# The delta-rule state loop of a hybrid decoder layer: three chained products a chunk replaced by one product with precomputed 128-row maps

## The chip, the cores and the metric

The kernel runs on one core of a Trainium2 chip. The metric is the device time of one execution in microseconds (us); the median of three runs of the kernel before is 1048.08 us (1046.65 to 1048.11). Traces name the engines PE (TensorE, matrix products; PEld is its weight load), DVE (VectorE), ACT (ScalarE), POOL (GpSimd) and SP (SyncE, which issues transfers).

## What is computed

One layer on 512 tokens of width 2048, all in float32: RMSNorm, one wide input projection into three groups of heads, an output projection, and the residual sum. The change touches the first group only, 12 heads of 64 channels with a state of 64 x 64 each. Cut to what matters:

```
h = rms(x, norm_g);  pa, pb, pc = split(h @ w_in)
r, k, v, ga, wd, ad = split(token_shift(pa, mu_a))   # RWKV-7 heads
# kk: normalized key, a: rate in (0,1), w: decay; per head and token t:
sa    = -state @ kk_t
state = state * w_t + outer(sa, kk_t * a_t) + outer(v_t, k_t)
y_t   = state @ r_t
# then a norm over the 64 channels of a head, a bonus term, and a silu gate
# pb: causal pooling; pc: stick-breaking attention (q, k, v, gate)
out = x + concat(ya, yb, yc) @ w_out
```

## The kernel before

Nearly all of TensorE's work is dense: the input projection is made tile by tile (54 tiles of 128 columns after a first group of three), each from 16 blocks of the inner dimension, and every block takes three products of 128 x 128 weights with 512 tokens (high part by high part, high by low, low by high). In the trace these products write `pj`; those of the output projection at the end write `oacc`. ACT and DVE make the two parts `wh` and `wl` of each half tile of weights while the half before it is used.

Everything else is put between these dense products. The RWKV heads (in six pairs, `rwkv(p)`), the attention (`attention(p)`) and the pooling are Python generators. After each dense product `pump` asks each generator whether its next small product may be issued. The answer comes from a planner, `Pace`, which estimates when operands will be ready, and adds a margin: `MARGIN` (2.5) in general and `TIGHT` in the state loop. The order of TensorE's instructions is therefore fixed when the program is built; if the estimate was too early, TensorE stops at the small product until its operand is there, since products run in order. Vector work under `urgent()` is moved ahead in DVE's queue.

A pair's 512 tokens are eight chunks of 64. For each pair:

- Products of the keys `bk` with `amr` (decayed keys and, in its third and fourth part, decayed `r`) go to two `gm` banks, 8 products a half of the chunks; DVE masks them into `lt`, `amr` and `rx`.
- `lt` is inverted: 32 x 32 blocks go through DRAM, DVE substitutes row by row (`xblk`), and two rounds of small products (`q1`, `q2`) join the blocks. `done[("mid", p)]` then lets the next pair begin.
- `bk` is transposed to `bkt`, the values `v` to half of `uv`. The other half of `uv` holds the state.
- The state loop goes over the chunks. A chunk is three chained products (`wps`, `ups`, `sps`, all in one bank `wus`), each read by DVE before the next can run, and two products for the output `y`. POOL makes `se`, the decayed old state.

A bank of PSUM is taken by tag: `g` has three, `c` two, `y` one. `amr` and `lt` exist twice, for even and odd pairs.

Of the kernel before, what the change touches and what calls it, by code (L numbers as in the profile page):

```python
# [13 lines left out]
P = 128  # L14
# [39 lines left out]
MARGIN = 2.5  # L54
TIGHT = 0.5
AHEAD = 300
EVACUATE = 25
DL = 4.0
SCAN = 150
TP = 15  # L60

# [155 lines left out]
def hybrid_trunk_kernel(ctx: ExitStack, tc: tile.TileContext, x, xT, w_in, w_out, vecs, consts, up_w, pool_w, out):  # L217
# [79 lines left out]

    amr_flats = [rp.tile([P, NC_ * 4 * C], F32, tag=f"amr{i}", name=f"amr{i}") for i in range(2)]
    amrs = [a.rearrange("p (c a t) -> p c a t", c=NC_, a=4) for a in amr_flats]
    lt_flats = [rp.tile([P, NC_ * 2 * C], F32, tag=f"lt{i}", name=f"lt{i}") for i in range(2)]  # L300
# [17 lines left out]
    KQ = 4  # L318
    for pl, tag, parts in ((ap, "q2", 1), (ap, "k2", 1), (ap, "w30", 1), (rp, "bk", 2), (rp, "bkt", 2), (rp, "rx", 2),
                           (rp, "uv", 2), (None, "amr", 3), (ap, "w20", 1), (ap, "w21", 1)):  # L320
        if pl is None:
            xt = amr_flats[1][:, 0:parts * T].rearrange("p (k t) -> p k t", k=parts)
        else:
            xt = pl.tile([P, parts, T], F32, tag=tag, bufs=2 if tag in ("bk", "rx") else 1, name=name("x"))
# [67 lines left out]

    def need2(*tiles):
        def at():
            q = pace.slots.get("g", [])
            t = max([pace.ready.get(Pace.key(a), 0.0) for a in tiles] + [0.0])
            free = sorted([pace.read.get(k, 1e9) for k in q] + [0.0] * (BANKS["g"] - len(q)))
            return MARGIN + max(t, free[1])

        return at  # L400
# [151 lines left out]
    def rwkv(p):  # L552
        col = lambda v: vec[:, v + p:v + p + 1]
        amr_flat, amr, lt = amr_flats[p % 2], amrs[p % 2], lts[p % 2]
        while ("k", p) not in got or (p > 0 and not done.get(("mid", p - 1))):
            yield None
# [65 lines left out]

        rx = rp.tile([P, NC_, 2, C], F32, tag="rx", bufs=2, name=name("rx"))
        ms = strict.rearrange("p (o t) -> p o t", o=1)
        mi = incl.rearrange("p (o t) -> p o t", o=1)
        for half in range(2):
            cs = slice(4 * half, 4 * half + 4)
            yield need2(*([amr_flat, bk] if half == 0 else []))
            gs = [gb("gm"), gb("gm")]
            for j in range(4):  # L630
                cc = 4 * half + j
                for h, s, other in quad:
                    mm(gs[h][:, j * P:(j + 1) * P], bk[s, cc, :, :], amr[s, cc, h:4:2, :])
# [47 lines left out]

        yield soon(lt)


        xt = tmp("xt", NC_ * B)
        xt3 = xt.rearrange("p (c t) -> p c t", t=B)
        for h in range(2):
            dve.transpose(xt3[h * HD:h * HD + B], lt[h * HD:h * HD + B, :, h, 0:B])
        yield need(xt, tag="g")
# [6 lines left out]
        for h in range(2):  # L696
            r0 = h * HD + B
            dve.tensor_copy(out=w1[r0:r0 + B, :], in_=q1[r0:r0 + B, :NC_ * B])
        yield need(w1, tag="g")
# [5 lines left out]
        for h in range(2):  # L705
            r0 = h * HD
            dve.tensor_copy(out=lt[r0:r0 + B, :, h, B:C], in_=q2[r0:r0 + B, :NC_ * B].rearrange("p (c t) -> p c t", t=B))
# [6 lines left out]
        bkt = rp.tile([P, NC_, P], F32, tag="bkt", name=name("bkt"))  # L714
        for half in range(2):
            yield need(bk, tag="g")
            tr = gb("tr")
            for j in range(4):
                transpose(tr[:, j * P:(j + 1) * P], bk[:, 4 * half + j, :, :])
            act.copy(out=bkt[:, 4 * half:4 * half + 4, :], in_=tr.rearrange("p (c t) -> p c t", c=4))  # L720

# [18 lines left out]
        for cc in range(NC_):  # L740
            last = cc + 1 == NC_
            yield need(amr_flat, uv, tag="c", margin=TIGHT)
            wus = cb("wus")
            wps, ups, sps = wus[:, 0:P], wus[:, P:P + C], wus[:, 2 * P:3 * P]
            mm(wps, amr[:, cc, 0:2, :], uv[:, cc, :, :])
            wsb = rp.tile([P, C], F32, tag="wsb", bufs=2, name=name("wsb"))
            with urgent():
                dve.tensor_copy(out=wsb[lo, :], in_=wps[lo, 0:C])
                dve.tensor_copy(out=wsb[hi, :], in_=wps[hi, C:P])
                if not last:  # L750
                    se = rp.tile([P, C], F32, tag="se", bufs=2, name=name("se"))
# [6 lines left out]
            yps = ybank[:, (cc % 4) * P:(cc % 4 + 1) * P]  # L758
# [5 lines left out]
            if not last:  # L764
                mm(sps, bkt[:, cc, :], uv[:, cc, :, :])
                with urgent():
# [204 lines left out]

    spare = [rp.tile([P, 2, T], F32R, tag=t, bufs=2, name=name("first")) for t in ("bk", "rx")]

# [24 lines left out]
    for h, s, other in quad:  # L998
        for i in range(2):
            pool.memset(amrs[i][other, :, 2 + h, :], 0.0)  # L1000
            pool.memset(lts[i][s, :, 1 - h, :], 0.0)

    def begin():
# [139 lines left out]
```

## Time and profile before

| | |
|---|---|
| median of 3 runs | 1048.08 us |
| the profiled execution's own time | 1047.92 us |
| span of its trace | 1046.1 us |
| PE busy | 990.5 us (95%) |
| DVE, ACT, POOL busy | 677.9, 500.4, 225.6 us |

A busy PE is counted by modelled ends of the products, which overlap: dense products are recorded with some 400 ns each, yet follow each other at some 230 ns. What the engine could still save is therefore read in two ways: from the distance between starts in the timeline, and from the list of waits.

### The profile page before, as it was taken

The page shows a single profiled execution, that of the slowest core. Times are in us where ns is not written, and L with a number is a line of the kernel's source. Part 1 is how long each engine was busy: PE and PEld are TensorE (multiplying, and loading weights), DVE is VectorE, ACT ScalarE, POOL GpSimd, SP SyncE. Part 2 cuts the span into 40 slices and gives each one's busy share as a digit, 9 for nine tenths or more (in the row PEclk, how much of TensorE's full clock was granted, in tenths as well). Part 3 has the DMA queues.
Part 4 walks back from the last instruction along what each step waited for, and adds up shares of the span by engine and source line. Part 5 has one row for each costly group of instructions (what it writes and reads, how often), then busy time and mean ns, then how long its engine had stood idle before and what let it go on. Part 6 is the DMA issues. An engine that isn't in the chain of part 4 may idle for free.

```text
span 1046.1 us, 13931 instructions
## 1 busy us (share of the span) xinstructions
PE 990.5 (95%) x5084; PEld 789.5 (75%) x5084; DVE 677.9 (65%) x1393; ACT 500.4 (48%) x814; POOL 225.6 (22%) x296
## 2 busy tenths in 40 slices
PE   8999999898998899988999999989899999999998
PEld 6867867677776777776877777767767877888886
DVE  5369685679668795687957888487974566323232
ACT  5656645554455653745645556556552226222111
POOL 0124320233212422233212232134221221000000
PEclk8999999999999999999999999999999999999999
DMA  9522323131231323113231322313232336724241
GB/s 336 197 86 78 100 82 99 64 88 61 91 103 45 90 74 124 62 66 86 66 121 61 96 66 91 106 60 77 78 101 77 111 107 219 257 104 141 101 141 61
DMA packets 62228, 109.18 MB, mean 104 GB/s; under 512 B 29776, under 2 KB 31184, under 8 KB 62160
## 3 DMA queue, kind: packets, MB, share of 16 engines
q1 hardware_dynamic: 62160, 108.30, 31.0%
q8 instruction: 40, 0.66, 0.3%
q14 instruction: 28, 0.23, 0.1%
HBM read 98.84 MB, written 9.44 MB: 104 GB/s over the span
## 4 chain that ended last, share of the span: by engine, by line
PE 45%; DVE 27%; issue 13%; ACT 7%; POOL 5%; DMA 3%; SPq 0%; POOLq 0%; DVEq 0%
PE pj L378 21%; PE oacc L378 16%; DVE wl L211 4%; POOL e L211 3%; DVE n L211 3%; DVE pr L211 3%; DVE xblk L211 2%; DVE uv L211 2%; DVE u L211 2%; PE first L378 2%; ACT e L211 2%; DVE amr L211 2%; DMA lt<-in_x 1%; DVE w L211 1%; PE o L378 1%
## 5 line engine op out<-in xcount | busy, mean ns | idle before, releaser
L378 PE MATMUL pj<-hh,wl 128*128 128x512 f32 x864 | 346.0, 401 | 5.7 <-DVE wl L211 5.6
L378 PE MATMUL pj<-hh,wh 128*128 128x512 f32 x864 | 346.6, 401 | 0.1
L378 PE MATMUL pj<-hl,wh 128*128 128x512 f32 x864 | 345.9, 400 | 0.0
L211 DVE TENSOR_TENSOR wl<-raw,wh 128x1024 fp32r<-128x1024 f32 x140 | 176.3, 1259 | 159.9 <-ACT wh L211 156.0
L211 ACT CAST wh<-raw 128x1024 fp32r<-128x1024 f32 x140 | 146.5, 1046 | 246.3 <-PE oacc L378 121.5
L378 PEld LDWEIGHTS pj<-hh,wl 128*128 128x128 f32 x864 | 163.0, 189 | 40.1 <-DVE wl L211 8.1
L378 PEld LDWEIGHTS pj<-hh,wh 128*128 128x128 f32 x864 | 163.0, 189 | 34.8 <-issue 3.3
L378 PEld LDWEIGHTS pj<-hl,wh 128*128 128x128 f32 x864 | 162.9, 189 | 32.4 <-issue 2.1
L378 PE MATMUL oacc<-wl,yh 128*128 128x512 f32 x256 | 100.0, 391 | 0.0
L378 PE MATMUL oacc<-wh,yh 128*128 128x512 f32 x256 | 99.6, 389 | 0.0
L378 PE MATMUL oacc<-wh,yl 128*128 128x512 f32 x256 | 99.6, 389 | 0.0
L211 POOL TENSOR_SCALAR e<-e 128x512 f32<-128x512 f32 x28 | 48.3, 1726 | 211.4 <-ACT e L211 165.6
L211 POOL TENSOR_SCALAR se<-uv,ec 64x64 f32<-64x64 f32 x84 | 56.4, 672 | 100.5 <-DVE uv L211 95.3
L211 POOL TENSOR_TENSOR d<-u 128x512 f32<-128x512 f32 x25 | 39.4, 1575 | 130.8 <-DVE u L211 93.9
L378 PEld LDWEIGHTS oacc<-wh,yl 128*128 128x128 f32 x256 | 48.1, 188 | 10.3 <-issue 0.2
L378 PEld LDWEIGHTS oacc<-wl,yh 128*128 128x128 f32 x256 | 48.1, 188 | 10.2 <-issue 0.2
L378 PEld LDWEIGHTS oacc<-wh,yh 128*128 128x128 f32 x256 | 48.1, 188 | 9.9
L211 DVE TENSOR_TENSOR_SCAN n<-n,m 128x512 f32<-128x512 f32 (+3 forms) x48 | 41.0, 864 | 15.8 <-ACT n L211 15.6
L211 ACT ACTIVATE e<-e 128x512 f32<-128x512 f32 x50 | 31.5, 629 | 36.2 <-POOL e L211 35.7
L211 DVE TENSOR_TENSOR u<-pj,rstd 128x512 f32<-128x512 f32 x50 | 34.5, 690 | 19.5 <-PE pj L378 18.6
L211 DVE TENSOR_TENSOR pr<-xblk,nblk 128x60 f32<-128x60 f32 (+8 forms) x180 | 42.1, 234 | 4.9
L211 DVE TENSOR_TENSOR xblk<-xblk,pr 128x60 f32<-128x60 f32 (+8 forms) x180 | 40.7, 226 | 4.6
(203 smaller groups left out, 1313.4 us busy)
## 6 DMA issues: line engine op xcount, KB each, us to landing
raw<-in_w_in SPq DMA_DIRECT2D x108, 512.0 KB, 3.4
raw<-in_w_out SPq DMA_DIRECT2D x32, 512.0 KB, 3.5
lt<-in_x SPq DMA_DIRECT2D x8, 512.0 KB, 3.7
xr<-in_x SPq DMA_DIRECT2D x16, 256.0 KB, 6.7
out<-xr SPq DMA_DIRECT2D x16, 256.0 KB, 4.4
yin<-yd SPq DMA_DIRECT2D x14, 256.0 KB, 4.0
fr<-in_w_in SPq DMA_DIRECT2D x12, 256.0 KB, 7.5
nblk<-s SPq DMA_DIRECT2D x24, 128.0 KB
```

The source lines that it names most:

```text
L211: return call(*args, **kw)
L378: pe.matmul(o, lhsT, rhs, start=start, stop=stop)
```

## The change

The inverse, the rates and the output products of a chunk are multiplied out ahead of the loop. `amr` is transposed (`amt`) and multiplied by the inverse `lt` (bank `am`, copied to `amx`). For each chunk and head `amx` is multiplied with a tile `bx` (banks `gh`), and DVE adds the result back into `bx`, on one half of the partitions to the transposed keys and the masked products, on the other half to the identity (now the third part of `amr`) and the decayed `r`. `bx` then holds two maps of 128 rows, one that takes state and values of a chunk to the next state and one that takes them to the output. The loop is one product `s`, one product for `y`, and a scaling by DVE; `wsb`, `se` and the copies of `uv` are gone.

`amr` now exists once; `done[("inv", p)]` lets the next pair begin, and `done[("mid", p)]` lets it write `amr` and `bk`. The margin `TIGHT` is 0.8 in place of 0.5, and the joining and the new products use `QUICK`, 1.0, in place of 2.5. An attention pair waits for the one before it.

```diff
-TIGHT = 0.5
+TIGHT = 0.8
+QUICK = 1.0
-TP = 15
+TP = 16
...
-        while ("k", p) not in got or (p > 0 and not done.get(("mid", p - 1))):
+        while ("k", p) not in got or (p > 0 and not done.get(("inv", p - 1))):
...
-        while p > 1 and not done.get(("rwkv", p - 2)):
+        while (p > 0 and not done.get(("mid", p - 1))) or (p > 1 and not done.get(("rwkv", p - 2))):
             yield None
...
-        dve.tensor_tensor(amr[lo, :, 2, :], r3[lo], e[lo, :, 1:], ALU.mult)
-        pool.tensor_tensor(amr[hi, :, 3, :], r3[hi], e[hi, :, 1:], ALU.mult)
+        dve.tensor_tensor(amr[:, :, 3, :], r3, e[:, :, 1:], ALU.mult)
...
+        for half in range(2):
+            yield need(bk, tag="g")
+            tr = gb("tr")
+            for j in range(4):
+                transpose(tr[:, j * P:(j + 1) * P], bk[:, 4 * half + j, :, :])
+            act.copy(out=bx[:, 4 * half:4 * half + 4, 0, :, :], in_=tr.rearrange("p (c h t) -> p c h t", c=4, h=2))
...
+        amt = rp.tile([P, NC_, P], F32, tag="bk", bufs=2, name=name("amt"))
+        for half in range(2):
+            yield need(amr_flat, tag="g")
+            tr = gb("at")
+            for j in range(4):
+                transpose(tr[:, j * P:(j + 1) * P], amr[:, 4 * half + j, 0:2, :])
+            act.copy(out=amt[:, 4 * half:4 * half + 4, :], in_=tr.rearrange("p (c t) -> p c t", c=4))
...
+        amx = rp.tile([P, NC_, P], F32, tag="bk", bufs=2, name=name("amx"))
+        for half in range(2):
+            yield need(lt, amt, tag="c", margin=QUICK)
+            g = cb("am")
+            for j in range(4):
+                cc = 4 * half + j
+                mm(g[:, j * P:(j + 1) * P], lt[:, cc, :, :], amt[:, cc, :])
+            act.copy(out=amx[:, 4 * half:4 * half + 4, :], in_=g.rearrange("p (c t) -> p c t", c=4))
+        for half in range(2):
+            cs = slice(4 * half, 4 * half + 4)
+            yield need2(amx, bx, tag="c", margin=QUICK)
+            gs = [cb("gh"), cb("gh")]
+            for j in range(4):
+                cc = 4 * half + j
+                for h, s, other in quad:
+                    mm(gs[h][:, j * P:(j + 1) * P], amx[s, cc, :], bx[s, cc, :, h, :])
+            with urgent():
+                for h, s, other in quad:
+                    g4 = gs[h].rearrange("p (c a t) -> p c a t", c=4, a=2)
+                    dve.tensor_tensor(bx[other, cs, :, h, :], g4[other], bx[other, cs, :, h, :], ALU.add)
+                    dve.tensor_tensor(bx[s, cs, :, h, :], g4[s], amr[s, cs, 2:4, :], ALU.add)
         done[("mid", p)] = True
...
-            yield need(amr_flat, uv, tag="c", margin=TIGHT)
-            wus = cb("wus")
-            wps, ups, sps = wus[:, 0:P], wus[:, P:P + C], wus[:, 2 * P:3 * P]
-            mm(wps, amr[:, cc, 0:2, :], uv[:, cc, :, :])
...
-                dve.tensor_copy(out=wsb[lo, :], in_=wps[lo, 0:C])
-                dve.tensor_copy(out=wsb[hi, :], in_=wps[hi, C:P])
...
-                        pool.tensor_scalar(se[s, :], uv[s, cc, h, :], ec[s, cc:cc + 1], None, ALU.mult)
-            yield need(wsb, lt, tag="y" if cc % 4 == 0 else None, margin=TIGHT)
-            mm(ups, lt[:, cc, :, :], wsb)
+            yield need(bx, uv, tag="y" if cc % 4 == 0 else None if last else "c", margin=TIGHT)
+            if not last:
+                sps = cb("s")
+                mm(sps[:, 0:P], bx[:, cc, 0, :, :], uv[:, cc, :, :])
+                with urgent():
                     for h, s, o in quad:
+                        dve.tensor_scalar(uv[s, cc + 1, h, :], sps[s, h * C:(h + 1) * C], ec[s, cc:cc + 1], None, ALU.mult)
...
-            mm(yps, uv[:, cc, :, :], amr[:, cc, 2:4, :], True, False)
-            with urgent():
-                dve.tensor_copy(out=uv[lo, cc, 0, :], in_=ups[lo, :])
-                dve.tensor_copy(out=uv[hi, cc, 1, :], in_=ups[hi, :])
-            yield need(uv, margin=TIGHT + 0.1)
-            if not last:
-                mm(sps, bkt[:, cc, :], uv[:, cc, :, :])
-                with urgent():
-                    for h, s, o in quad:
-                        dve.scalar_tensor_tensor(uv[s, cc + 1, h, :], sps[s, h * C:(h + 1) * C], ec[s, cc:cc + 1], se[s, :], ALU.mult, ALU.add)
-            mm(yps, uv[:, cc, :, :], rx[:, cc, :, :], False, True)
+            mm(ybank[:, (cc % 4) * P:(cc % 4 + 1) * P], uv[:, cc, :, :], bx[:, cc, 1, :, :])
```

How TensorE's instructions stand in the state loop before the change: from the third chained product of one chunk of pair 0 (`sps`, a part of the bank `wus`) to the first of the next (`wps`).

```order
L378 MATMUL wus_2091<-uv_1617,bkt_1603 128x128
L378 MATMUL y_2044<-rx_710,uv_1617 128x128
L378 MATMUL pj_2129<-hh_104,wh_2030 128x512
L378 MATMUL pj_2129<-hl_120,wh_2030 128x512
L378 MATMUL pj_2129<-hh_104,wl_2031 128x512
L378 MATMUL pj_2129<-hh_105,wh_2030 128x512
L378 MATMUL pj_2129<-hl_121,wh_2030 128x512
L378 MATMUL pj_2129<-hh_105,wl_2031 128x512
L378 MATMUL pj_2129<-hh_106,wh_2030 128x512
L378 MATMUL pj_2129<-hl_122,wh_2030 128x512
L378 MATMUL wus_2193<-uv_1617,amr_97 128x128
```

The same engine in the loop of the changed kernel, pair 1, a whole chunk.

```order
L380 MATMUL s_2989<-uv_2938,bx_1801 128x128
L380 MATMUL y_2993<-bx_1801,uv_2938 128x128
L380 MATMUL pj_2915<-hh_104,wl_2872 128x512
L380 MATMUL pj_2915<-hh_105,wh_2871 128x512
L380 MATMUL pj_2915<-hl_121,wh_2871 128x512
L380 MATMUL pj_2915<-hh_105,wl_2872 128x512
L380 MATMUL pj_2915<-hh_106,wh_2871 128x512
L380 MATMUL pj_2915<-hl_122,wh_2871 128x512
L380 MATMUL pj_2915<-hh_106,wl_2872 128x512
L380 MATMUL pj_2915<-hh_107,wh_2871 128x512
L380 MATMUL pj_2915<-hl_123,wh_2871 128x512
L380 MATMUL pj_2915<-hh_107,wl_2872 128x512
```

The row after these is the next chunk's `s`. Where eight dense products lay between one link of the chain and the next (nine at the other two links of a chunk), ten now do, and a chunk has one link in place of three.

DVE in the loop before the change, pair 0: one chunk's copies and its update of the state (each written x2, once for each head), with other work between them.

```order
L211 COPY wsb_2019<-wus_2017 64x64 x2
L211 TENSOR_TENSOR wl_2031<-raw_2028,wh_2030 128x1024
L211 COPY uv_1617<-wus_2017 64x64 x2
L211 SCALAR_TENSOR_TENSOR n_2005<-n_2005,m_2006 128x512
L211 TENSOR_TENSOR w_2000<-w_2000,n_2005 128x512
L211 SCALAR_TENSOR_TENSOR uv_1617<-wus_2017,ec_653,se_2022 64x64 x2
```

DVE in the changed kernel between the first and the second group of `gh` products of pair 1.

```order
L212 TENSOR_TENSOR wl_2872<-raw_2869,wh_2871 128x1024
L212 TENSOR_TENSOR e_2780<-e_2780,d_2141 128x512
L212 TENSOR_TENSOR bx_1801<-gh_2880,bx_1801 64x8x64
L212 TENSOR_TENSOR bx_1801<-gh_2880,amr 64x8x64
L212 TENSOR_TENSOR bx_1801<-gh_2881,bx_1801 64x8x64
L212 TENSOR_TENSOR bx_1801<-gh_2881,amr 64x8x64
L212 SCALAR_TENSOR_TENSOR qs_2799<-qm_2853,qs_2799 128x512
L212 SCALAR_TENSOR_TENSOR u_2788<-u_2788,vec,y_463_2856 128x512
L212 TENSOR_TENSOR bk_2951<-e_2780,e_2751 64x8x64
L212 TENSOR_TENSOR ck_2798<-u_2788,qs_2799 128x512
L212 TENSOR_TENSOR u_2913<-pj_2790,rstd 128x512
L212 TENSOR_TENSOR wl_2919<-raw_2916,wh_2918 128x1024
```

Six short instructions a chunk have left the loop, and four adds of 64 x 512 stand in one block behind each `gh` group, ahead of the next `wl`.

## Rows read from the trace of the kernel before

**Rows 1.** The page: span, and busy time of each engine with its share.

```profile
span 1046.1 us, 13931 instructions
...
PE 990.5 (95%) x5084; PEld 789.5 (75%) x5084; DVE 677.9 (65%) x1393; ACT 500.4 (48%) x814; POOL 225.6 (22%) x296
```

**Rows 2.** Waits of PE: who waited for whom, us in total, times, longest.

```profile
PE wus L378 <- DVE uv L211: 26.0, 24, 2.2
PE wus L378 <- DVE wsb L211: 6.4, 9, 1.2
PE pj L378 <- DVE wl L211: 5.6, 5, 1.9
...
PE y L378 <- DVE uv L211: 1.0, 1, 1.0
```

**Rows 3.** Timeline of PE, 314 to 320 us: start, us, instruction [idle before].

```profile
314.25 0.40 PE L378 MATMUL pj<-hh,wh 128*128 128x512 f32 x1
314.48 0.33 PE L378 MATMUL wus<-wsb,lt 128*128 128x64 f32 x2
314.64 0.44 PE L378 MATMUL y<-amr,uv 128*128 128x128 f32 x2
314.84 0.47 PE L378 MATMUL pj<-hl,wh 128*128 128x512 f32 x1
315.15 0.39 PE L378 MATMUL pj<-hh,wl 128*128 128x512 f32 x1
...
316.77 0.40 PE L378 MATMUL pj<-hh,wh 128*128 128x512 f32 x1
319.12 0.49 PE L378 MATMUL wus<-uv,bkt 128*128 128x128 f32 x2 [1.95 <-DVE uv L211]
```

**Rows 4.** Timeline of DVE in the same stretch.

```profile
316.70 1.22 DVE L211 TENSOR_TENSOR_SCAN c<-fresh,e 128x512 f32<-128x512 f32 x1
317.84 0.72 DVE L211 SCALAR_TENSOR_TENSOR sq<-d,vec,sq 128x512 f32<-128x512 f32 x1
318.59 0.47 DVE L211 COPY uv<-wus 64x64 f32<-64x64 f32 x2
```

**Rows 5.** Timeline of PE around four transposes of 128 x 128.

```profile
300.69 0.39 PE L378 MATMUL pj<-hh,wl 128*128 128x512 f32 x1
300.92 0.60 PE L382 MATMUL vt<-kon,d 128*128 128x128 f32 x4
...
301.59 0.39 PE L378 MATMUL qm<-sh,bmean_r 128*128 128x512 f32 x1
```

**Rows 6.** Timeline of PE around eight products of 64 rows each.

```profile
98.53 0.39 PE L378 MATMUL pj<-hh,wl 128*128 128x512 f32 x1
98.85 1.16 PE L378 MATMUL gm<-amr,bk 64*128 64x128 f32 x16
99.94 0.50 PE L378 MATMUL pj<-hh,wh 128*128 128x512 f32 x1
100.28 0.39 PE L378 MATMUL pj<-hl,wh 128*128 128x512 f32 x1
```

**Rows 7.** Groups of DVE by form: count, busy us, mean ns, idle before.

```profile
L211 DVE TENSOR_TENSOR wl<-raw,wh 128x1024 fp32r<-128x1024 f32 x140 | 176.3, 1259 | 159.9 <-ACT wh L211 156.0 <-PE pj L378 3.2
...
L211 DVE SCALAR_TENSOR_TENSOR uv<-wus,ec,se 64x64 f32<-64x64 f32 x84 | 23.7, 282 | 7.2 <-PE wus L378 5.2
L211 DVE COPY wsb<-wus 64x64 f32<-64x64 f32 x96 | 21.2, 220 | 17.9 <-PE wus L378 16.8
L211 DVE COPY uv<-wus 64x64 f32<-64x64 f32 x96 | 21.2, 220 | 7.0 <-PE y L378 4.9
...
L211 DVE TENSOR_TENSOR amr<-sq,E 64x512 f32<-64x512 f32 x12 | 10.5, 871 | 0.2
...
L211 DVE TENSOR_TENSOR q<-cq,q 64x512 fp32r<-64x512 f32 x12 | 8.2, 686 | 1.0 <-ACT q L211 0.7
```

**Rows 8.** Group of ACT: copies out of a bank of transposes.

```profile
L211 ACT COPY bkt<-tr 128x512 f32<-128x512 f32 x12 | 6.6, 589 | 14.4 <-PE tr L382 14.4
```

More of the change, by code (lines that the diff above doesn't have):

```diff
@@ L294, in load_constants @@
         dve.tensor_scalar(nvec[:, 12:13], vec[:, V_QN:V_QN + 1], HD ** -0.5, None, ALU.mult)
-    amr_flats = [rp.tile([P, NC_ * 4 * C], F32, tag=f"amr{i}", name=f"amr{i}") for i in range(2)]
-    amrs = [a.rearrange("p (c a t) -> p c a t", c=NC_, a=4) for a in amr_flats]
+    amr_flat = rp.tile([P, NC_ * 4 * C], F32, tag="amr", name="amr")
+    amr = amr_flat.rearrange("p (c a t) -> p c a t", c=NC_, a=4)
     lt_flats = [rp.tile([P, NC_ * 2 * C], F32, tag=f"lt{i}", name=f"lt{i}") for i in range(2)]
@@ L318, in hybrid_trunk_kernel @@
     KQ = 4
-    for pl, tag, parts in ((ap, "q2", 1), (ap, "k2", 1), (ap, "w30", 1), (rp, "bk", 2), (rp, "bkt", 2), (rp, "rx", 2),
+    for pl, tag, parts in ((ap, "q2", 1), (ap, "k2", 1), (ap, "w30", 1), (rp, "bk", 2), (rp, "bx", 4),
                            (rp, "uv", 2), (None, "amr", 3), (ap, "w20", 1), (ap, "w21", 1)):
         if pl is None:
-            xt = amr_flats[1][:, 0:parts * T].rearrange("p (k t) -> p k t", k=parts)
+            xt = amr_flat[:, 0:parts * T].rearrange("p (k t) -> p k t", k=parts)
         else:
-            xt = pl.tile([P, parts, T], F32, tag=tag, bufs=2 if tag in ("bk", "rx") else 1, name=name("x"))
+            xt = pl.tile([P, parts, T], F32, tag=tag, bufs=2 if tag in ("bk", "bx") else 1, name=name("x"))
         k = len(xk)
@@ L391, in need, with need2 @@
         return at
-    def need2(*tiles):
+    def need2(*tiles, tag="g", margin=MARGIN):
         def at():
-            q = pace.slots.get("g", [])
+            q = pace.slots.get(tag, [])
             t = max([pace.ready.get(Pace.key(a), 0.0) for a in tiles] + [0.0])
-            free = sorted([pace.read.get(k, 1e9) for k in q] + [0.0] * (BANKS["g"] - len(q)))
-            return MARGIN + max(t, free[1])
+            free = sorted([pace.read.get(k, 1e9) for k in q] + [0.0] * (BANKS[tag] - len(q)))
+            return margin + max(t, free[1])
         return at
@@ L553, in rwkv @@
         col = lambda v: vec[:, v + p:v + p + 1]
-        amr_flat, amr, lt = amr_flats[p % 2], amrs[p % 2], lts[p % 2]
-        while ("k", p) not in got or (p > 0 and not done.get(("mid", p - 1))):
+        lt = lts[p % 2]
+        while ("k", p) not in got or (p > 0 and not done.get(("inv", p - 1))):
             yield None
@@ L620, in rwkv @@
         yield soon(rs)
-        rx = rp.tile([P, NC_, 2, C], F32, tag="rx", bufs=2, name=name("rx"))
+        bx = rp.tile([P, NC_, 2, 2, C], F32, tag="bx", bufs=2, name=name("bx"))
         ms = strict.rearrange("p (o t) -> p o t", o=1)
@@ L632, in rwkv @@
                 for h, s, other in quad:
-                    mm(gs[h][:, j * P:(j + 1) * P], bk[s, cc, :, :], amr[s, cc, h:4:2, :])
+                    mm(gs[h][:, j * P:(j + 1) * P], bk[s, cc, :, :], amr[s, cc, h:4:3 - h, :])
             for h, s, other in quad:
@@ L682, in rwkv @@
         yield soon(lt)
+        done[("inv", p)] = True
         xt = tmp("xt", NC_ * B)
         xt3 = xt.rearrange("p (c t) -> p c t", t=B)
-        for h in range(2):
-            dve.transpose(xt3[h * HD:h * HD + B], lt[h * HD:h * HD + B, :, h, 0:B])
-        yield need(xt, tag="g")
+        with urgent():
+            for h in range(2):
+                dve.transpose(xt3[h * HD:h * HD + B], lt[h * HD:h * HD + B, :, h, 0:B])
+        yield need(xt, tag="g", margin=QUICK)
         q1 = gb("q1")
@@ L695, in rwkv @@
                 mm(q1[r0 + B:r0 + 2 * B, cc * B:(cc + 1) * B], lt[r0:r0 + B, cc, h, B:C], xt3[r0:r0 + B, cc, :])
[L696 to L699, printed above, removed]
+        with urgent():
+            for h in range(2):
+                r0 = h * HD + B
+                dve.tensor_copy(out=w1[r0:r0 + B, :], in_=q1[r0:r0 + B, :NC_ * B])
+        yield need(w1, tag="g", margin=QUICK)
         q2 = gb("q2")
@@ L704, in rwkv @@
                 mm(q2[r0:r0 + B, cc * B:(cc + 1) * B], w1[r0 + B:r0 + C, cc * B:(cc + 1) * B], lt[r0 + B:r0 + C, cc, h, B:C])
-        for h in range(2):
-            r0 = h * HD
-            dve.tensor_copy(out=lt[r0:r0 + B, :, h, B:C], in_=q2[r0:r0 + B, :NC_ * B].rearrange("p (c t) -> p c t", t=B))
+        with urgent():
+            for h in range(2):
+                r0 = h * HD
+                dve.tensor_copy(out=lt[r0:r0 + B, :, h, B:C], in_=q2[r0:r0 + B, :NC_ * B].rearrange("p (c t) -> p c t", t=B))
+        amx = rp.tile([P, NC_, P], F32, tag="bk", bufs=2, name=name("amx"))
[14 more added lines that the diff above has]
+                    mm(gs[h][:, j * P:(j + 1) * P], amx[s, cc, :], bx[s, cc, :, h, :])
+            with urgent():
+                for h, s, other in quad:
+                    g4 = gs[h].rearrange("p (c a t) -> p c a t", c=4, a=2)
+                    dve.tensor_tensor(bx[other, cs, :, h, :], g4[other], bx[other, cs, :, h, :], ALU.add)
+                    dve.tensor_tensor(bx[s, cs, :, h, :], g4[s], amr[s, cs, 2:4, :], ALU.add)
         done[("mid", p)] = True
@@ L711, in rwkv @@
             yield None
[L714 to L720, printed above, removed]
         while ("v", p) not in got:
@@ L741, in rwkv @@
             last = cc + 1 == NC_
-            yield need(amr_flat, uv, tag="c", margin=TIGHT)
-            wus = cb("wus")
-            wps, ups, sps = wus[:, 0:P], wus[:, P:P + C], wus[:, 2 * P:3 * P]
-            mm(wps, amr[:, cc, 0:2, :], uv[:, cc, :, :])
-            wsb = rp.tile([P, C], F32, tag="wsb", bufs=2, name=name("wsb"))
-            with urgent():
-                dve.tensor_copy(out=wsb[lo, :], in_=wps[lo, 0:C])
-                dve.tensor_copy(out=wsb[hi, :], in_=wps[hi, C:P])
-                if not last:
-                    se = rp.tile([P, C], F32, tag="se", bufs=2, name=name("se"))
+            yield need(bx, uv, tag="y" if cc % 4 == 0 else None if last else "c", margin=TIGHT)
+            if not last:
+                sps = cb("s")
+                mm(sps[:, 0:P], bx[:, cc, 0, :, :], uv[:, cc, :, :])
+                with urgent():
                     for h, s, o in quad:
-                        pool.tensor_scalar(se[s, :], uv[s, cc, h, :], ec[s, cc:cc + 1], None, ALU.mult)
-            yield need(wsb, lt, tag="y" if cc % 4 == 0 else None, margin=TIGHT)
-            mm(ups, lt[:, cc, :, :], wsb)
+                        dve.tensor_scalar(uv[s, cc + 1, h, :], sps[s, h * C:(h + 1) * C], ec[s, cc:cc + 1], None, ALU.mult)
             if cc % 4 == 0:
                 ybank = bank("y", "y")
-            yps = ybank[:, (cc % 4) * P:(cc % 4 + 1) * P]
-            mm(yps, uv[:, cc, :, :], amr[:, cc, 2:4, :], True, False)
-            with urgent():
-                dve.tensor_copy(out=uv[lo, cc, 0, :], in_=ups[lo, :])
-                dve.tensor_copy(out=uv[hi, cc, 1, :], in_=ups[hi, :])
-            yield need(uv, margin=TIGHT + 0.1)
-            if not last:
-                mm(sps, bkt[:, cc, :], uv[:, cc, :, :])
-                with urgent():
-                    for h, s, o in quad:
-                        dve.scalar_tensor_tensor(uv[s, cc + 1, h, :], sps[s, h * C:(h + 1) * C], ec[s, cc:cc + 1], se[s, :], ALU.mult, ALU.add)
-            mm(yps, uv[:, cc, :, :], rx[:, cc, :, :], False, True)
+            mm(ybank[:, (cc % 4) * P:(cc % 4 + 1) * P], uv[:, cc, :, :], bx[:, cc, 1, :, :])
             if cc % 4 == 3:
@@ L797, in attention @@
     def attention(p):
+        while p > 0 and not done.get(("att", p - 1)):
+            yield None
         qk = []
@@ L969, in finish @@
             got[(kind, i)] = u
-    spare = [rp.tile([P, 2, T], F32R, tag=t, bufs=2, name=name("first")) for t in ("bk", "rx")]
+    spare = [rp.tile([P, 2, T], F32R, tag=t, bufs=2, name=name("first")) for t in ("bk",)] + [rp.tile([P, 4, T], F32R, tag="bx", bufs=2, name=name("first"))]
     def first_home(i):
@@ L999, in hybrid_trunk_kernel @@
         for i in range(2):
-            pool.memset(amrs[i][other, :, 2 + h, :], 0.0)
             pool.memset(lts[i][s, :, 1 - h, :], 0.0)
+        one = ident[s, h * C:(h + 1) * C].rearrange("p (o t) -> p o t", o=1)
+        pool.tensor_copy(out=amr[s, :, 2, :], in_=one.to_broadcast([C, NC_, C]))
     def begin():
```

2 lines of the change are left out of this document (1 added, 1 removed).

## The prediction

> **What bounds the kernel now.** First the busy times: PE is busy 990.5 of 1046.1 us, no other engine over 65% [rows 1]. So a gain must come out of PE's stream: fewer us of products in it, or fewer stops. Busy time cannot tell the first, so I read starts in the timeline. Dense products follow each other every 0.23 us (314.25 to 314.48), although each is recorded with some 0.4 us [rows 3]. Whatever is put between them costs what it adds to that distance.
>
> For the stops I read PE's list of waits. The two products of the loop that wait for the copied values wait 26.0 us in 24 places and 6.4 us in 9, and a product for `y` 1.0 us in one: 33.4 us in 34 waits. The next in size is the dense stream's own wait for `wl`, 5.6 us in 5 [rows 2]. The view's other rows are one or two places each with 3.1 us or less; neither `q` of the joining nor `oacc` of the output projection is among them.
>
> One wait read closely: the dense product before it starts at 316.77, so without a wait the next would start at 317.00; it starts at 319.12, which is 2.12 us late, while the row counts 1.95 as idle, since the modelled end of the product before hides the rest [rows 3]. DVE shows why: `uv` was to be copied after a scan of 1.22 us and another operation of 0.72 us, and came at 318.59 [rows 4]. The planner had put the product where DVE would be free on its estimate, and DVE was not. I add the hidden 0.17 us to each of the 34 waits: 33.4 + 5.8 = 39.2 us, 1.15 us a wait. The loop has 23 links a pair from product through DVE to product (three a chunk, less the last), 138 in all, so a link costs 0.28 us on average.
>
> **The products.** The loop's small float32 products cost 0.22 us each: two of them between dense ones move the starts from 314.25 to 315.15, 0.90 us where two distances would be 0.46 [rows 3]; the one with 64 columns is no cheaper there. Each of the 48 chunks loses three of its five: 144 x 0.22 = 31.7 us out of the stream.
>
> Added are three kinds. (1) Transposes of `amr`, 12 groups of four: four take 301.59 - 300.69 - 0.46 = 0.44 us [rows 5], so 5.3 us. (2) `am`, 48 full float32 products: 48 x 0.22 = 10.6 us. (3) `gh`, 12 groups of eight products of 64 rows, alternating between the upper and the lower half of the rows as `gm` does. The trace has `gm` for this: eight cost 100.28 - 98.53 - 0.46 = 1.29 us [rows 6], so 12 x 1.29 = 15.5 us. The transposes of `bk` only move. Together +31.4 us.
>
> So the products come out at -0.3 us: what the loop saves is spent on preparing it. The third kind is the only doubtful price. One after another, eight at 0.22 would be 1.76 us, 5.6 us more over the 12 groups; at half of that, 0.88 us, they would be 4.9 us less. I take 1.29, the row of the same shapes in the same alternation. The Trainium skill, TensorEngine Tiling (Array Packing), section Tiling Modes, says that tiles on different rows run in parallel and that a change of the tiling mode drains the engine: by its first half alone the sum would go by 0.88 us a group and be 4.9 us lower, by both it is between; the row, with its late first start (98.85 instead of 98.76) and its late return, decides.
>
> **The stops in the loop.** Of 138 links, 42 remain (seven a pair; the last chunk makes no state). Before, a link had eight dense products and two small ones to hide in (8 x 0.23 + 0.44 = 2.28 us), nine and one (2.29) or nine and two (2.51), by the order of the instructions; now it has ten and two, 2.74 us. That is 0.23 to 0.46, on average 0.38 us more for DVE to come in. Each of 34 waits shorter by 0.38 leaves 39.2 - 12.9 = 26.3 us on 138 links, 0.19 us a link, and 42 x 0.19 = 8.0 us. DVE's part in a link is much the same: two copies of 220 ns or two updates of 282 ns before, two scalings of a size between them now [rows 7]. Bounds: 0, and 42 x 0.28 = 11.8 us.
>
> **The new stops ahead of the loop.** Five links a pair now run on a margin of 1.0 or 0.8: `q1` to `q2`, `q2` to `am`, `am` to the first `gh`, first to second `gh`, second `gh` to the loop; 30 in all. The first of these existed and never waited, with a margin of 2.5. Bounds: nothing, or a full wait of 1.15 us on each, 34.5 us. The last two kinds (12 links) have a block of four adds inside. An add of 64 x 512 is bounded by 686 and 871 ns [rows 7]; I take the first, the mean of the group where nothing stretches it, so a block is 2.74 us after 1.29 us of products, inside some 20 dense products (4.6 us) at the first of the two. There I take the old loop's 0.28 us. At the other 18, DVE has two copies with half an add's columns each (under 686 ns) or ACT two copies of 589 ns [rows 8], and the order gives 10 to 20 dense products (2.3 to 4.6 us), so I take half. 12 x 0.28 + 18 x 0.14 = 5.9 us.
>
> **What I cost at nothing.** DVE loses 96 + 96 copies and 84 updates, 66.1 us [rows 7], and gains 48 adds (32.9 us) and 84 scalings (18.5 to 23.7 us): a little less on an engine 65% busy. What stands behind an add is the next `wl`, a rival below. POOL loses its `se`; no wait of PE ends on POOL. ACT gains 24 copies of 589 ns, 14.1 us on an engine 48% busy [rows 1, 8]; the 12 of `amx` stand in a link priced above, the other 12 wait for nothing near. A single `amr` makes the next pair's masks wait for `mid` of this one: covered by the span of a pair, in which the loop gets much shorter; if it were not, the next pair's loop would slip under later tiles, and only the last pair's could reach the output. First loads in other pieces, attention one after another, one more temporary: no wait of PE hangs on them.
>
> **The sum.** -0.3 for products, -39.2 + 8.0 for the loop's stops, +5.9 for new stops: -25.6 us. The profiled execution took 1047.92 us, so 1022.3; it lies 0.16 us under the median of 1048.08, so the forecast is 1022.5 us, 2.4% faster. That the state loop is one product a chunk saves hardly any product time; the gain is 96 links less to stop at.
>
> **Rivals.**
>
> *Almost no stops are left.* With the longer hiding time, links rarely wait: -0.3 - 39.2 leaves 1008.6 us. For it: the joining never waited. Against: in the wait above DVE was held 1.9 us by two other operations [rows 4], and such runs remain.
>
> *The stops move to the preparation.* Each of the 12 links with adds waits a full 1.15 us, the 18 others 0.28, and the loop keeps 8.0: 13.8 + 5.0 + 8.0 = 26.8, -0.3 - 39.2 + 26.8 = -12.7, 1035 us. For it: the planner reckons the four urgent adds as if they ran side by side, so it is early by up to three adds, 2.06 us, where nothing else lies between. Against: the order has some 20 dense products between the groups.
>
> *The adds make `wl` late, and the kernel slower.* The four adds are urgent and wait in DVE's queue for the products; the `wl` behind them, 1259 ns [rows 7], is needed every 24 dense products (5.5 us), and its buffer comes free only one half tile ahead. If the whole block falls on the dense stream, 12 x 2.74 = 32.9 us are added, 1055 us. It decides from 25.6 / 12 = 2.13 us a group upward; at 2.0 to 2.3 there is no change. For it: PE already waits for `wl` 5 times [rows 2]. Against: these are 5 of 140, and in the order a `wl` stands ahead of each block. The Trainium skill, TensorEngine Tiling (Array Packing), section PSUM Bottleneck, speaks for this one: tiling speeds up the products, not the taking of their results out of PSUM.
>
> *The change does not do what it says*: the loop's links do not fall. The order excludes that; what can fail is only the price of `gh`, 5.6 us, which lies within the forecast's own range.
>
> **Chances and range.** The forecast with its own range of 1012 to 1032: 0.62. Almost no stops, below 1012: 0.12. Stops in the preparation, 1032 to 1046: 0.14. No change within 0.2% (2.1 us, about what a measurement of this kernel can tell): 0.04. Slower through late `wl`: 0.08. So faster 0.88, same 0.04, slower 0.08. A range of 1010 to 1040 leaves out the lower half of the second case and the upper third of the third with the last two, about 0.2.
>
> **What would show it.** Waits of PE on the loop's product `s` in about 7 places in place of 34, 7 us by the list; waits at `am`, `gh` and `q` few; PE's busy time about 990 us still, and the span shorter by the stops. Eight `gh` at a cost near 1.3 us, four transposes near 0.44, `s` and `y` together 0.44. Wrong would be: long waits of `gh` or the first `s` for the adds, more waits of `pj` for `wl` than 10 us, or `gh` near 1.76 us.

## The result, and the profile after

The changed kernel takes 1033.92 us (median of four runs, 1031.8 to 1034.42) against 1047.37 us for the kernel before (four runs): a ratio of 0.9871, 95% interval 0.985 to 0.9893. It is faster by 13.5 us, where 25.6 were forecast. The rows below are of the execution at 1034.42 us.

The page, with span and busy times, to be held against [rows 1]:

```profile
span 1032.6 us, 13786 instructions
...
PE 989.5 (96%) x5132; PEld 791.3 (77%) x5132; DVE 660.9 (64%) x1249; ACT 512.0 (50%) x838; POOL 151.8 (15%) x204
```

The waits of PE, to be held against [rows 2]:

```profile
PE pj L380 <- DVE wl L212: 14.0, 14, 2.1
PE s L380 <- DVE uv L212: 6.9, 7, 2.6
PE gh L380 <- DVE bx L212: 3.5, 5, 1.3
...
PE pj L380 <- ACT wh L212: 2.4, 2, 2.0
...
PE y L380 <- DVE uv L212: 1.3, 1, 1.3
```

PE is as busy as before; it stands less. The loop's 33.4 us in 34 waits have become 8.2 in 8 (`s` and `y` on `uv`). But the largest row is now one that the sum had left alone: the dense stream waits 16.4 us in 16 places for its weights `wl` and `wh`, where it waited 5.6 us in 5.

The price that was called doubtful, eight `gh` products in the timeline of PE:

```profile
187.18 0.39 PE L380 MATMUL pj<-hl,wh 128*128 128x512 f32 x1
187.49 1.16 PE L380 MATMUL gh<-bx,amx 64*128 64x128 f32 x16
188.59 0.50 PE L380 MATMUL pj<-hh,wl 128*128 128x512 f32 x1
188.92 0.39 PE L380 MATMUL pj<-hh,wh 128*128 128x512 f32 x1
```

188.92 - 187.18 - 0.46 = 1.28 us, as `gm` in [rows 6] had it (1.29).

One of the new waits, in PE's timeline:

```profile
267.94 0.40 PE L380 MATMUL pj<-hh,wh 128*128 128x512 f32 x1
268.18 0.40 PE L380 MATMUL pj<-hl,wh 128*128 128x512 f32 x1
270.71 0.51 PE L380 MATMUL pj<-hh,wl 128*128 128x512 f32 x1 [2.13 <-DVE wl L212]
...
272.28 0.63 PE L380 MATMUL pj<-hh,wl 128*128 128x512 f32 x1
272.70 0.63 PE L380 MATMUL pj<-hh,wh 128*128 128x512 f32 x1
273.13 0.63 PE L380 MATMUL pj<-hl,wh 128*128 128x512 f32 x1
```

The stop of 2.13 us is followed, 1.6 us later, by dense products that start every 0.43 us in place of 0.23, from 272.28 to 275.26 us. The windows of this place have the reason in the column PEclk (after the busy times of PE, PEld, DVE, ACT and POOL): the granted clock is 0.50, 1.2 of 2.4 GHz.

```profile
270.00:271.50 1.50, 0.79 (x3) 0.68 (x4) 1.50 (x3) 0.63 (x2) 0.80 (x1) 1.00 0.00 0
...
272.50:275.00 2.50, 2.50 (x7) 1.92 (x7) 1.80 (x5) 1.68 (x4) 0.00 (x0) 0.50 0.29 107
```

Away from the start there are five such stretches, 17.1 us in all (windows of 1 us, each counted as twice what the clock lacks to 1); before there was one, 3.4 us.

What was DVE doing while `wl` was awaited? Its timeline:

```profile
262.59 1.22 DVE L212 TENSOR_TENSOR_SCAN n<-n,m 128x512 f32<-128x512 f32 x1
263.72 0.18 DVE L212 TENSOR_TENSOR pr<-xblk,nblk 128x42 f32<-128x42 f32 x1
...
264.52 0.20 DVE L212 TENSOR_TENSOR xblk<-xblk,pr 128x42 f32<-128x42 f32 x1
...
267.79 0.95 DVE L212 TENSOR_TENSOR_SCAN n<-n,m 128x384 f32<-128x384 f32 x1
268.65 2.00 DVE L212 TENSOR_TENSOR wl<-raw,wh 128x1024 fp32r<-128x1024 f32 x1
```

It works without a gap on the substitution (`xblk`, `pr`), the attention's scans and `wl`. No `gh` add is near: the `gh` groups of this kernel stand at 187 to 194, 317 to 323 us and so on, while 12 of the 16 waits for weights lie inside the substitution of a pair (pair 1's, for one, runs from 240 to 271 us) and three more within 6 us behind one.

DVE was as full there before. Pair 1's substitution lay at 240 to 267 us then (third busy time: DVE):

```profile
240.00:250.00 10.00, 8.26 (x42) 6.40 (x40) 8.93 (x38) 2.48 (x4) 0.57 (x3) 1.00 0.15 52
250.00:260.00 10.00, 9.04 (x45) 7.34 (x45) 9.58 (x27) 7.91 (x15) 4.67 (x7) 1.00 0.15 53
```

Over all six substitutions DVE was busy 92% of 183 us before, and is 91% of 167 us now. What changed is what runs beside it. Before, the loop of one pair reached 7 to 14 us into the substitution of the next, with 1.8 to 2.7 us of stops there in each of five; now its last `s` lies 13 to 24 us ahead, and no stop of the loop falls there. Pair 0's substitution has no loop beside it in either kernel, and there PE waits for `wl` alike: 2.2 us in 2 before, 2.6 in 2 now. The growth, from 3.4 to 13.8 us for weights, is at the five later pairs.

**An account by starts.** For each two neighbours in PE's timeline I take the distance of their starts less the typical one of their kinds; what is over goes to the listed wait, if there is one, or to the clock, if the window has a low one. First to last product:

| us | before | after | change | forecast |
|---|---|---|---|---|
| stops of the loop (34, now 8) | 38.2 | 9.0 | -29.2 | -31.2 |
| new stops ahead of the loop (7) | 0 | 5.9 | +5.9 | +5.9 |
| dense stream for `wl`, `wh` (5, now 16) | 6.4 | 19.0 | +12.6 | 0 |
| low clock | 1.7 | 7.6 | +5.9 | 0 |
| other listed stops | 11.4 | 8.0 | -3.4 | 0 |
| everything else | 982.9 | 977.9 | -5.0 | -0.3 |
| sum | 1040.6 | 1027.4 | -13.2 | -25.6 |

The two terms on which the forecast stood came out; two that it lacked, 18.5 us together, took them back. The -5.0 is in the main late starts in the loop too short to be listed (some 5 us before, 1 now; the figure hangs on what is taken as typical) and the shorter half-rate stretch at the start (3.4 us in place of 6.8, so 1.7).

### The profile page after: what moved, and what is told of

The parts are those of the page before. It is cut to its first block, busy times and chain, and to the rows that moved or that the text cites. A ratio compares the mean times of both kernels' runs of the same rounds, so it can differ in the third digit from the quotient of the medians.

```text
span 1032.6 us, 13786 instructions
## 1 busy us (share of the span) xinstructions
PE 989.5 (96%) x5132; PEld 791.3 (77%) x5132; DVE 660.9 (64%) x1249; ACT 512.0 (50%) x838; POOL 151.8 (15%) x204
## 4 chain that ended last, share of the span: by engine, by line
PE 39%; DVE 29%; issue 15%; ACT 8%; POOL 5%; DMA 2%; SPq 0%; POOLq 0%; DVEq 0%
PE oacc L380 17%; PE pj L380 16%; DVE wl L212 5%; DVE xblk L212 3%; DVE pr L212 3%; DVE n L212 3%; DVE bx L212 3%; POOL e L212 2%; ACT e L212 2%; PE first L380 2%; ACT n L212 2%; DVE u L212 1%; DVE amr L212 1%; DVE w L212 1%; ACT wh L212 1%
## 5 line engine op out<-in xcount | busy, mean ns | idle before, releaser
L212 POOL TENSOR_SCALAR e<-e 128x512 f32<-128x512 f32 x28 | 45.0, 1607 | 200.1 <-ACT e L212 183.9
L212 ACT ACTIVATE e<-e 128x512 f32<-128x512 f32 x50 | 31.5, 630 | 33.4 <-POOL e L212 33.1
L212 POOL CAST kl<-klo 64x512 fp32r<-64x512 f32 x24 | 20.9, 869 | 168.9 <-DVE klo L212 124.1
```

The source lines that it names most:

```text
L212: return call(*args, **kw)
```

## The experiments

The theory: PE's 34 stops had been time in which DVE and ACT caught up. With the stops gone, PE asks for weights sooner, and DVE, full in the substitution, makes `wl` late there. The rivals: the block of `gh` adds makes `wl` late; or the gain is the larger margin's, not the chain's.

### The margin alone, and the chain alone

```diff
 x1, the kernel before:
-TIGHT = 0.5
+TIGHT = 0.8
 x2, the changed kernel:
-TIGHT = 0.8
+TIGHT = 0.5
```

> The kernel before with the loop's margin 0.8 in place of 0.5, nothing else. Theory (fewer links; a part of every removed stop is given back where the dense stream then waits for its weights): each of the 34 loop waits gets up to 0.4 us shorter, so the list shows some 22 us of loop waits in place of 33; half of that comes back as waits of pj for wl or wh; about 1042 us. Rival (the margin is the gain, not the number of links): loop waits below 13 us in the list and about 1034 us, the time of the changed kernel.

> The changed kernel with the loop's margin back at 0.5: eight dense products a link in place of ten. Theory (fewer links): 42 links with 0.46 us less to hide in wait some 4 us more in sum, 12 to 14 us of waits of s in the list, and the time is 1035 to 1038 us. Rival (the margin is the gain): at least 1044 us.

Measured: 1038.66 us for x1 (ratio 0.9921, 0.9906 to 0.9935) and 1045.56 us for x2 (0.9982, 0.997 to 0.9994), beside 1047.52 us before. The waits of x1:

```profile
PE wus L378 <- DVE uv L211: 18.2, 23, 2.2
PE wus L378 <- DVE wsb L211: 12.5, 13, 2.6
PE pj L378 <- DVE wl L211: 2.9, 3, 1.9
```

and of x2:

```profile
PE pj L380 <- DVE wl L212: 16.4, 16, 1.6
PE s L380 <- DVE uv L212: 13.4, 5, 2.7
```

At the same `TIGHT` the new chain is worth only 2 us (0.5) or 5 us (0.8). Fewer links do cut the loop's waits at equal margin, 33.4 to 13.4 us, as the theory had it for x2, but the time is the rival's. The gain is given back in two parts: 17.6 us of waits for weights (1.2 of them on `wh`) in place of 5.6, and ten low-clock stretches, 34 us at half the clock and so up to 17 us lost, in place of one. The larger margin gains 9 us in the old loop, but not as either expectation had it: its waits stay at 31.6 us in 38 places (with two on `y`, 0.9 us), though ten dense products lie in each link. All its listed waits together fall from 51.1 to 43.8 us: 1.8 in the loop, 2.7 for weights, the rest elsewhere.

The five waits of x2 are the second link of pairs 0 to 4. DVE's timeline ahead of the one at 332.59 us:

```profile
327.41 0.69 DVE L212 TENSOR_TENSOR bx<-gh,amr 64x512 f32<-64x512 f32 x1
...
329.93 0.75 DVE L212 SCALAR_TENSOR_TENSOR m<-d,vec,e 128x512 f32<-128x512 f32 x1
330.71 0.28 DVE L212 TENSOR_SCALAR uv<-s,ec 64x64 f32<-64x64 f32 x1
330.91 1.21 DVE L212 TENSOR_TENSOR wl<-raw,wh 128x1024 fp32r<-128x1024 f32 x1
332.15 0.29 DVE L212 TENSOR_SCALAR uv<-s,ec 64x64 f32<-64x64 f32 x1
```

Here the adds, the next pair's masks that waited for `mid`, and a `wl` between the two halves of the scaling do hold the loop: the queue behind the `gh` groups is a place of its own, at one link a pair.

### Less work for DVE in the substitution

```diff
-            dve.tensor_tensor(prv, xblk[:, 0:ni, j:j + 1]...
-            dve.tensor_tensor(xblk[:, 0:ni, j + 1:B], ...
+            if j % 2 == 0:
+                pace.record(...)   # both operations, for the planner alone
+            else:
+                dve.tensor_tensor(prv, xblk[:, 0:ni, j:j + 1]...
+                dve.tensor_tensor(xblk[:, 0:ni, j + 1:B], ...
```

Every second of the 30 substitution steps is left out, some 6.6 us of DVE a pair, in the changed kernel (x3) and the one before (x4). The planner still reckons with them, so PE's order stays.

> The changed kernel without every second step of the substitution of the 32 x 32 blocks (its output is not the layer's then); the planner still reckons them, so PE's order is that of the changed kernel. DVE loses 180 instructions of some 0.23 us, 41 us. Theory (the dense stream waits for wl and wh because DVE is full in the stretch of the substitution): the 16.4 us of waits of pj for wl and wh fall to some 6, the stretches at half the clock to 2 or fewer, and the time to about 1022 us. Rival (the blocks of urgent adds make wl late): these waits stay at 14 us or more, at least 1030 us.

> The kernel before without the same steps of the substitution. Theory (its stops in the loop gave DVE and ACT the time to catch up, so it hardly waits for wl): waits of pj for wl fall by no more than 4 us, loop waits by a few us, about 1042 us, so that the difference of the two kernels grows from 13 to some 20 us. Rival (the weights are late for a reason that both share): it gains as much as the changed kernel does, and the difference stays near 13 us.

Measured: 1013.24 us for x3 (0.9678, 0.9661 to 0.9694), 1038.99 us for x4 (0.9916, 0.9897 to 0.9936). x3's waits:

```profile
PE s L380 <- DVE uv L212: 8.2, 9, 2.6
PE pj L380 <- DVE wl L212: 4.6, 6, 1.0
PE gh L380 <- DVE bx L212: 3.5, 5, 1.4
```

The waits for weights fall from 16.4 to 5.2 us (with 0.6 on `wh`), low-clock stretches from five to two, and the loop's and the adds' waits stay. x4 has no wait for `wl` at all. So DVE's load in the substitution is what makes `wl` late, and the adds are not. x3 is 9 us faster than expected: against the changed kernel, an account by starts has 12.7 us less for weights and some 5 less of low clock. The difference of the two kernels is now 25.8 us, more than the 20 expected. That it is the forecast's size is in part luck: x3 still loses some 6 us for weights where x4 loses none, and about as much comes back in short late starts of the loop, which the sum did not have.

### One more buffer for the weights

```diff
-        wh = wp.tile(..., tag="wh", name=name("wh"))
-        wl = wp.tile(..., tag="wl", name=name("wl"))
+        wh = wp.tile(..., tag="wh", bufs=3, name=name("wh"))
+        wl = wp.tile(..., tag="wl", bufs=3, name=name("wl"))
...
-TP = 16
+TP = 13
```

x12 has the second part alone, as a control.

> The changed kernel with three buffers in place of two for each of `wh` and `wl` (and 13 in place of 16 buffers for temporaries, to make room); TensorE's order is that of the changed kernel but for one product at the start. Theory: `wl` is late because DVE is full for some 10 us in the substitution and can have made only one half tile ahead; with one half tile more (5.5 us) it works the backlog off earlier. Then the dense stream's waits for `wl` and `wh` fall from 16.4 us to under 6, the half-rate stretches behind them go too, and the time is 1018 to 1026 us. Rival: lead is not what is missing, because the order of DVE's queue, not the buffer, decides when `wl` is made: waits stay above 12 us, time 1031 to 1036.

> The control of the run with the third weight buffers: the changed kernel with 13 in place of 16 buffers for temporaries and nothing else; TensorE's order is the same. If the waits of the transposes `wT` in that run (14 us) come from the missing temporaries, they are here too, and the time is over 1038 us; if they come from `wl` being made earlier than the attention's scans, they are not: 1033 to 1036 us, with the waits for `wl` of the changed kernel.

Measured: 1037.12 us for x5 (0.9913, 0.99 to 0.9925), 1034.51 us for x12 (0.9891, 0.9872 to 0.991). x12 is the changed kernel, waits too (14.1 us in 15 for `wl`, 1.0 in 2 for `wT`). x5's list has no row for `wl` or `wh` any more; in their place stand:

```profile
PE s L380 <- DVE uv L212: 7.7, 9, 2.3
PE wT L384 <- ACT w L212: 7.6, 5, 2.9
PE wT L384 <- issue: 6.6, 3, 4.2
```

The theory of x5 had the waits for weights right and the time wrong; the rival had both wrong. More lead removes every wait for the weights, and PE then runs ahead to the next product that hangs on DVE in the same stretch, a transpose of the attention's `w`, which ACT makes from what DVE has made. By starts, 19 us of stops for weights go and 16 us of other stops come. The windows of the changed kernel say why lead does not help:

```profile
240.00:250.00 10.00, 9.08 (x42) 7.18 (x41) 9.38 (x28) 6.35 (x13) 2.31 (x4) 1.00 0.28 102
...
260.00:270.00 10.00, 7.40 (x35) 5.65 (x33) 9.38 (x27) 4.13 (x7) 1.99 (x3) 1.00 0.14 53
```

DVE is 64% busy over the span and 94% in these two windows of a substitution (85% in the one between): there it has hardly any room, and whichever of its results PE reaches first is the one waited for.

### DVE's load given to other engines

```diff
 x6, the changed kernel:
-    dve.tensor_scalar(uv[s, cc + 1, h, :], sps[...], ec[s, cc:cc + 1], None, ALU.mult)
+    act.activation(uv[s, cc + 1, h, :], sps[...], AF.Copy, scale=ec[s, cc:cc + 1])
 x11, the kernel before (wsb and uv, both halves):
-    dve.tensor_copy(out=wsb[lo, :], in_=wps[lo, 0:C])
+    act.copy(out=wsb[lo, :], in_=wps[lo, 0:C])
 x8, the changed kernel, q = 768:
-    dve.tensor_tensor(wl, raw, wh.bitcast(F32), ALU.subtract)
+    dve.tensor_tensor(wl[:, :q], raw[:, :q], wh.bitcast(F32)[:, :q], ALU.subtract)
+    pool.tensor_tensor(wl[:, q:], raw[:, q:], wh.bitcast(F32)[:, q:], ALU.subtract)
```

> The changed kernel with the loop's 84 scalings of the state on ACT in place of DVE; TensorE's order is the same. If what is left of the loop's stops (6.9 us in 7 waits on `s`) is DVE's queue, ACT at 50% takes them with fewer: under 3 us, and 1028 to 1031 us, with the waits for `wl` as before (they lie in other stretches). Rival: ACT's queue, with exponentials of 0.6 us and casts `wh` of over 1 us, is no freer where the loop needs it: 7 us of waits or more, and a time of 1033 to 1040.

> The kernel before with the 192 copies of the loop (values and products) on ACT in place of DVE; its 84 updates stay on DVE. It asks whether the gain of ACT in the loop needs the new chain. If the old loop's 33.4 us of stops are DVE's queue alone, ACT takes the 96 links that end on copies with half of that: 1030 to 1036 us. Rival: a chain of 138 links pays at every one whatever the engine, and ACT's 0.31 us a copy is longer than DVE's 0.22: 30 us of stops or more, 1043 to 1052 us.

> The changed kernel with the last 256 of 1024 columns of each `wl` made by POOL (15% busy) instead of DVE: DVE loses about 0.3 us in each of 140, some 41 us. Theory: the dense stream waits for DVE's load, so waits on `wl` fall from 14.0 us to under 8, 1024 to 1029 us. Rival: POOL takes 0.7 to 0.9 us for its quarter and stands behind its own operations of 1.6 us, so `wl` is later than before in more places: waits of 20 us or more, 1040 us and above.

Measured: 1026.13 us for x6 (0.9806, 0.9793 to 0.9818), 1036.06 us for x11 (0.9903, 0.9886 to 0.992), 1046.96 us for x8 (1.0004, 0.9994 to 1.0015). Waits of x6:

```profile
PE pj L380 <- DVE wl L212: 16.6, 16, 2.2
...
PE s L380 <- ACT uv L212: 2.8, 3, 2.0
```

x6 is the fastest kernel here that computes the whole layer, 20.4 us under the one before. PE's order by the names in its trace is the changed kernel's. The waits for weights are not fewer (19.0 us in 18, from 16.4 in 16), the loop's fall from 8.2 to 2.8 us, and only one low-clock stretch is left (3.4 us). So most of what remained of the loop's stops was the wait in DVE's queue: from the end of an `s` to its scaling the median is 1.3 us in the changed kernel and 0.4 in x6. But not all of the 8 us are the loop's. The granted clock of x6's four runs is 0.995 to 0.998 where the changed kernel's is 0.990 to 0.993, a difference of half a per cent or some 5 us, and none of the five low-clock stretches there lay right behind a stop of the loop. The old chain gains 10 us with its copies on ACT, much as the theory had it, in another order of PE's products, since the planner sees ACT; its loop waits go to 20.5 us in 25, most of it in these two rows:

```profile
PE wus L378 <- DVE uv L211: 14.1, 16, 1.8
PE wus L378 <- ACT uv L211: 4.8, 6, 1.5
```

With each loop partly on ACT the new chain is 10 us ahead. In x8 waits for `wl` are 13.1 us in 10, those of the loop 12.7 in 9 with one of 4.6: POOL needs 1218 ns for its 256 columns, DVE still 1063 ns for 768, and nothing is won. The time is the rival's, its 20 us of waits for `wl` are not there; PE's order is another one too, so x8 tells little of `wl` alone.

### Two that changed nothing, and a longer margin

```diff
 x9, the changed kernel (x10: x6 with the same):
-    m = ap.tile([P, 512], F32, tag="m", bufs=1, ...)
+    m = ap.tile([P, 512], F32, tag="m", bufs=2, ...)
-TP = 16
+TP = 15
 x7, the changed kernel:
-TIGHT = 0.8
+TIGHT = 1.2
```

> The changed kernel with two buffers in place of one for the attention's temporary `m` (and 15 in place of 16 buffers for other temporaries); TensorE's order is the same. In the substitution of the changed kernel ACT waits up to 3.33 us to write `m`, since DVE's scan of the one before has not run, and the next `wh` stands behind it. Theory: part of the lateness of `wl` comes through `wh`; with two, the waits of the dense stream for `wl` and `wh` fall from 16.4 us by about a third, to 9 to 12, and the time to 1027 to 1031 us. Rival: DVE alone is late (its queue, whatever ACT does): waits within 2 us of 16.4 and the time within 2 us of 1034.

> The changed kernel with the loop's scalings on ACT and the second `m` at once (15 buffers for other temporaries). The loop's stops and the stops for the weights lie in different stretches of a pair, so by the theory the gains add: 1026 less what the second `m` alone gains, about 1020 to 1023 us. Rival: both act on the same half-rate stretches, which are gone with the first, so that no more than 1 us is added: 1025 to 1027.

> The changed kernel with the margin of the loop at 1.2 in place of 0.8: about 12 dense products between links instead of ten. If the margin is what the loop's last stops lack, waits on `s` fall from 6.9 us to under 3 and the half-rate stretch behind them goes: 1027 to 1031 us. Rival, from the run of the old chain with the larger margin, whose loop waits hardly fell: they stay near 7 us, and the time moves only by how other work shifts, within 3 us of 1034.

Measured: 1035.27 us for x9 (0.989, 0.9873 to 0.9908), 1027.63 us for x10 (0.9825, 0.9804 to 0.9846), 1040.74 us for x7 (0.9952, 0.9935 to 0.9968). With a second `m` the waits for weights are 16.2 us in 15 in x9 and 19.1 in 19 in x10: the rival had it, ACT's wait was not what delayed `wl`. At a margin of 1.2 the loop's waits are 6.7 us in 6, no better; those for `wl` are 19.9 us and there are seven low-clock stretches, so it loses 7 us, more than the rival allowed. Longer links are thus not what the last stops lack; why 0.8 is better than 1.2 for the rest of the order is not shown.

## Why the prediction was half right

- **The products (-0.3)** held: `gh` 1.28 us, `s` with `y` 0.45, four transposes 0.45, eight `am` 1.79. The Trainium skill, TensorEngine Tiling (Array Packing), section Tiling Modes, has different tiles work in parallel, and a drain at a change of the tiling mode. The trace agrees with the row of `gm`, above the 0.88 us that the prediction estimated for the first alone.
- **The loop (-39.2 + 8.0)** held in size: 9.0 us left in 8 places. Its working did not: "each of 34 waits shorter by 0.38" fails in x1, where the old chain with the longer cover keeps its waits, so that the size came out is in part luck. What counts is links (x2), and which queue serves them (x6).
- **The new stops ahead of the loop (+5.9)** held: 5.9 us in 7. They did not become the second rival's 18.8. That the time, 1033.92 us, lies outside the forecast's own 1012 to 1032 and close to that rival's 1035 is a coincidence. At the old margin (x2) the queue behind the adds does hold the loop.
- **The step that failed** is the one headed "What I cost at nothing": DVE was called "a little less on an engine 65% busy". That share is a mean over stretches. In the substitutions DVE is busy some 91% of the time, as it already was in the trace of the kernel before, where the loop of the pair before still ran beside them. This adds 12.6 us for weights and, behind stops of several kinds, 5.9 us of low clock. The sum had late weights only as a rival with another cause, the `gh` adds; its own sign, over 10 us of `pj` for `wl`, came true (14.0), at the substitution instead. x3 against x4 shows the cause: with DVE relieved there, waits for weights fall to 5.2 us and to none, and the difference of the kernels grows from 13.5 to 25.8 us.
- What stays open: whether it was the loop's stops or its products beside a substitution that gave DVE the time before; the other listed stops (-3.4); the new margin `QUICK`, the single `amr` and the attention pairs one after another, which no run takes alone; and why some stops are followed by a low clock and others are not.

## What to carry to other kernels

Before a gain is booked for stops taken out of the bounding engine, look at the others stretch by stretch, not over the span: an engine at 64% that is above 90% where the bounding one will now arrive earlier takes gain back, and the trace of the kernel before already shows it. More buffers only moved the wait to the next result of the engine that is behind; less work on it there removed it. A short link of a chain can go to the engine with the shorter queue (84 instructions of 64 x 64: 5 us of stops). Compare a new structure with the old one at the same tuning: of 13.5 us here, 2 to 5 were the chain's at equal margin.

## What the runs showed of the hardware

The granted clock fell to half behind a stop in one kernel and not behind the same stop in another. In the changed kernel PE stopped 1.99 us for `wh` and 0.63 us for `wl` in pair 4's substitution, and the dense products behind start every 0.43 us:

```profile
632.74 0.50 PE L380 MATMUL pj<-hh,wh 128*128 128x512 f32 x1 [1.99 <-ACT wh L212]
...
634.10 0.80 PE L380 MATMUL pj<-hh,wl 128*128 128x512 f32 x1 [0.63 <-DVE wl L212]
...
635.98 0.63 PE L380 MATMUL pj<-hl,wh 128*128 128x512 f32 x1
636.40 0.63 PE L380 MATMUL pj<-hh,wl 128*128 128x512 f32 x1
```

In x6 the same products stopped 1.94 and 0.63 us, and those behind start every 0.23 us:

```profile
626.17 0.50 PE L380 MATMUL pj<-hh,wh 128*128 128x512 f32 x1 [1.94 <-ACT wh L212]
...
627.54 0.50 PE L380 MATMUL pj<-hh,wl 128*128 128x512 f32 x1 [0.63 <-DVE wl L212]
...
629.25 0.39 PE L380 MATMUL pj<-hl,wh 128*128 128x512 f32 x1
629.48 0.40 PE L380 MATMUL pj<-hh,wl 128*128 128x512 f32 x1
```

The number of such stretches also differs between kernels with PE's order and waits alike: five in the changed kernel, two (6.8 us) in x12, whose own four runs have granted clocks of 0.987 to 0.997 and times 4.7 us apart. A gain of a few us that comes from them alone is therefore not to be counted on.

The `wl` at 268.65 us took 2.00 us where the one at 261.08 took 1.22. Beside it POOL ran a subtraction and a selection, which took 1.24 us where 24 of its shape take 407 ns in the mean:

```profile
268.01 1.56 POOL L212 TENSOR_TENSOR d<-u 128x512 f32<-128x512 f32 x1 [8.17 <-DVE u L212]
...
269.57 1.24 POOL L212 TENSOR_SCALAR_AFFINE_SELECT w<-w 128x128 f32<-128x128 f32 x1
```

Work on POOL beside DVE can thus stretch either. Of the 140 `wl` of this trace the 102 with nothing on POOL beside them took 1.23 us at most, the other 38 took 1.35 us in the mean and up to 2.10. This fits x8, where a quarter of the columns less saved DVE 15%.
